# Three raw tiles and seven pairs of weight parts where one stream runs, and the next stage's first weights split on VectorE

## The chip, the cores and the metric

The kernel runs on one core of one Trainium2 chip. The metric is the device time of one execution in microseconds (us), the median of several runs. The matmul engine is TensorE (PE in the profile), the elementwise engines are VectorE (DVE), ScalarE (ACT) and GpSimd (POOL), and SyncE (SP) issues the loads of weights.

## The reference, cut to what matters

Two transformer blocks follow each other on `x` (512 tokens of 1024 features). Each has two layers, and each layer has two halves: token mixing, then a feed-forward. Every half has the same outline, and the change touches its joints:

```python
# first block, layer i (even: window and neighbourhood attention, odd: differential attention)
hx = hx + gx1 * yx                                    # yx = mixed @ w_out
hx = hx + gx2 * _mlp(_modulate(hx, norm2_g[i], sx2, cx2), mlp_w1[i], mlp_w2[i])
if with_ctx:                                          # layer 0 alone: a second stream, the context
    hc = hc + gc1 * yc
    hc = hc + gc2 * _mlp(_modulate(hc, norm2_g[i], sc2, cc2), mlp_w1[i], mlp_w2[i])
...
return _rms_norm(hx, final_g)                         # first block's end
# second block, layer l
h = _rmsnorm(x, norm1_w[l]) * (1.0 + sc1) + sh1
x = x + g1 * _token_mixers(h, w_in[l], ..., w_out[l])
h = _rmsnorm(x, norm2_w[l]) * (1.0 + sc2) + sh2
x = x + g2 * _conv_ffn(h, w_up[l], conv_f_w[l], w_down[l])
```

So a product (`@ w_out`, `@ w_down`, `@ mlp_w2`) ends in a residual add, the sum is normalised and modulated, and the next product (`@ mlp_w1`, `@ w_in`, `@ w_up`) starts from that. The norm needs all 1024 features of a token.

## The kernel before

Activations lie transposed: 8 chunks of 128 features by 512 tokens. A product in fp32 is made of three matmuls per chunk (`mm3`, L147 to L149): weights and activations are both split into a high part and a low part, and hi·hi, hi·lo and lo·hi are added in PSUM. A weight block of 1024 by 128 is loaded into a raw tile (`wraw`, 4 KB a partition), ScalarE writes its high part (`whi`, L129) and another engine subtracts for the low part (`wlo`, L130): VectorE, unless `weight()` is given another engine. A block is 24 matmuls of 512 columns. `whi` and `wlo` together are called a pair here. The pool of weights has a fixed number of raw tiles and of pairs; SP's load into a raw tile waits until the split that last used it is done, and a split waits until the matmuls that last used the pair are done.

`out_half` opens such a pool (`b.weights(env.wx, ...)`, L1489) while the last blocks of a layer's out-projection are still to be computed. The pool lasts through the feed-forward of that layer and the first blocks of the layer behind it. Loads of the modulation's weights (`w_ada`, used by VectorE at L181) take raw tiles of it too.

A joint of two stages is cut into two segments of 256 tokens, so that the norm of one can run beside products of the other:

- `down()` computes its last four blocks (three in the out-projection of the second block) segment by segment. Each output goes from PSUM into the residual `hx` (L154 on VectorE). After the four of segment 0, `norm` of segment 0 starts, while PE computes segment 1's four outputs.
- `norm`: squares on ScalarE (L213), added up on POOL (five) and VectorE (two, L218), a mean by matmul (`ms`, L224), a first root on ScalarE (`nr`, L232), a Newton step on VectorE (L233, L234, L235), then per chunk of features `nw` on VectorE (L242), the high part `axh` on ScalarE (L243) and the low part `axl` on VectorE (L244). At the end of the first block the final norm comes on top (L263 to L272, and a second Newton step).
- `first_chunks()` takes the first four blocks of the next product (called f0 to f3 below; g0, g1, ... are the blocks behind them), all four on segment 0 and then all four on segment 1, with `norm` of segment 1 between. The four are split with GpSimd as the engine.

There are five such joints with one stream: **A**, odd layer's out-projection to its MLP; **B**, that MLP to the first mixers (with the final norm); **C** and **E**, the mixers' out-projection to the conv FFN of layers 0 and 1; **D**, the first conv FFN to the second mixers. Which instruction stands where on an engine is decided by a scheduler when the program is built; each engine then runs its list in order.

Of the kernel before, what the change touches and what calls it, by code (L numbers as in the profile page):

```python
# [49 lines left out]
def segments(streams):  # L50
    return [(s, slice(i, i + SEG)) for s in reversed(streams) for i in range(0, s.n, SEG)]


class Build:
# [115 lines left out]
    def ada(self, w, bias, chunks, outs):  # L170

        nc = self.nc

        loaded = []

        def chunk(j):
            if loaded:
                raw, i = loaded.pop()
                for c, out in outs:
                    junk = self.tile(self.adap, [P, D], BF16, "adaj")  # L180
                    nc.vector.tensor_tensor_reduce(junk, raw, c, 1.0, self.vec(bias)[:, i:i + 1], ALU.mult, ALU.add,  # L181
                                                   out[:, i:i + 1])
            if j is not None:
                raw = self.wtile("wraw").rearrange("p a b -> p (a b)")
                nc.sync.dma_start(raw, self.io[w][j])
                loaded.append((raw, j))

        self.bg += [lambda j=j: chunk(j) for j in [*chunks, None]]
# [57 lines left out]
    def norm(self, pool, pp, s, sl, mod, outs, i, final=None):  # L246


        nc = self.nc
        scale, shift = mod  # L250
        h = s.h[:, :, sl]
        chunk = lambda k: h[:, k]
        acc = self.squares(pool, SEG, chunk, sq=f"sq{i}", pool_adds=5)
        if final is not None:
            acc2 = self.squares(pool, SEG, chunk, sq=f"sr{i}", pool_adds=5, scale=final)
        yield
        ms = self.mean(pp, acc, SEG)
        if final is not None:
            ms2 = self.mean(pp, acc2, SEG)
        r = self.newton(pool, ms, SEG)  # L260
        if final is not None:
            m = self.tile(pool, [P, SEG], F32, "nms")
            nc.vector.tensor_tensor(m, r, r, op=ALU.mult)  # L263
            nc.vector.tensor_tensor(m, m, ms2, op=ALU.mult)
            r2 = self.newton(pool, m, SEG)
            nc.vector.tensor_tensor(r2, r2, r, op=ALU.mult)
        for k in range(KC):
            hi, lo = outs[s.key][k]
            self.scaled(pool, h[:, k], r if final is None else r2, scale[:, k:k + 1], shift[:, k:k + 1], hi[:, sl], lo[:, sl])
        if final is not None:  # L270
            for k in range(KC):
                nc.vector.scalar_tensor_tensor(h[:, k], h[:, k], final[:, k:k + 1], r, op0=ALU.mult, op1=ALU.mult)  # L272
# [83 lines left out]
def first_chunks(b, pp, srcs, parts, streams, norm):  # L356


    ws = [b.weight(src, e=b.nc.gpsimd) for src, _ in srcs]
    ps = [{s.key: b.tile(pp, [P, T], F32, "dd") for s in streams if s.key in keys} for _, keys in srcs]  # L360
    for s, sl in segments(streams):
        for w, p in zip(ws, ps):
            if s.key in p:
                b.mm3(p[s.key][:, sl], w, parts[s.key], sl=sl)
            if norm:
                norm = norm()
    return [{k: v[:, :T if k == "x" else TC] for k, v in p.items()} for p in ps]


def down(b, pp, src, ops, streams, gates, kc=KC, ms=range(KC), after=None):  # L370


    ms = list(ms)
    full = ms[:-TAIL] if after else ms
    for m in full:
        w = b.weight(src(m), kc)
        for s in streams:
            ps = b.tile(pp, [P, T], F32, "dd")[:, :s.n]
            b.mm3(ps, w, ops[s.key], range(kc))
            b.add(s, m, slice(0, s.n), ps, gates[s.key])  # L380
    ws = [(m, b.weight(src(m), kc)) for m in ms[len(full):]]
    then = None
    for i, (s, sl) in enumerate(segments(streams) if ws else ()):
        for m, w in ws:
            ps = b.tile(pp, [P, T], F32, "dd")[:, :SEG]
            b.mm3(ps, w, ops[s.key], range(kc), sl)
            b.add(s, m, sl, ps, gates[s.key])
            if then:
                then = then()
        then = after(i, s, sl)  # L390
    return then
# [12 lines left out]
def mlp(b, pp, layer, a, norm, hset, streams, gates):  # L404

    nc, io = b.nc, b.io
    keys = [s.key for s in streams]
    up = lambda j: io[f"mlp_w1_{layer}"][j]
    first = first_chunks(b, pp, [(up(j), keys) for j in range(TAIL)], a, streams, norm)
    ctx = ExitStack()  # L410
    mt = b.pool(ctx, "mt", hset.side)
# [35 lines left out]
class EvenAttention:  # L447
# [6 lines left out]
    def load(self):  # L454

        b, ip = self.b, self.ip
        nc, io = b.nc, b.io
        b.rope_tables(b.cp)
        for n, w in (("maskA", 3 * P), ("maskB", 7 * P)):
            self.mask[n] = b.tile(ip, [P, w], F32R, n)  # L460
            for o in range(0, w, TA):
                m = slice(o, min(o + TA, w))
                raw = b.tile(ip, [P, TA], F32, "raw")[:, :m.stop - o]
                nc.sync.dma_start(raw, io[n][:, m])
                nc.scalar.copy(self.mask[n][:, m], raw)
        self.sink = b.tile(ip, [P, 8], F32, "sink")
        nc.sync.dma_start(self.sink, io["a_sink"].broadcast_to([P, 8]))
# [841 lines left out]
def conv_ffn(b, pp, l, a, norm, hset, streams, gates):  # L1309
    nc, io = b.nc, b.io  # L1310
    cw = b.vec(f"conv_f_w_{l}")
    up = lambda ch: io[f"w_up_{l}"][ch]
    chs = (0, NFF, 1, NFF + 1)
    first = dict(zip(chs, first_chunks(b, pp, [(up(ch), ["x"]) for ch in chs], a, streams, norm)))
    ctx = ExitStack()
    ft = b.pool(ctx, "ft", hset.side)
# [158 lines left out]
def out_half(b, env, w_out, ops, slots, streams, gates, mods, conds=(), order=range(KC), load=None, ada=None):  # L1475


    early = []
    for m, ps in enumerate(slots):
        w = b.weight(w_out[m])  # L1480
        for key, p in ps.items():
            b.mm3(p, w, ops[key], order)
    env.att.close()
    if load:
        load()
    streams = streams()
    env.new = b.open_set(env.other, [s.key for s in streams])
    env.wx, env.pdx = ExitStack(), ExitStack()
    b.weights(env.wx, b.nm("wd"), 4, 4, env.other)  # L1489
    for m, ps in enumerate(slots):  # L1490
        for s in streams:
            b.add(s, m, slice(0, s.n), ps[s.key], gates[s.key])
    env.ppx.close()
    env.pp = b.pool(env.pdx, "pd", space=PSUM)
    b.hold = 16
    env.wax.close()
    env.cond = None
    if conds:
        env.cond, c = b.open_cond(env.ins.side, conds)
        ada(*c)  # L1500
    rest = lambda after: down(b, env.pp, lambda m: w_out[m], ops, streams, gates, ms=range(len(slots), KC), after=after)
    return streams, *norms(b, env.pp, env.new, mods, streams, env.ins.side, rest)


def norms(b, pp, pset, mods, streams, side, rest, final=None):

    out = {}
    ctx = ExitStack()
    pool = b.pool(ctx, "nrm", side)
    b.bufs.update({"nr0": 2, "nt": 2})  # L1510

    def norm(i, s, sl):
        if not out:
            out.update(pset.all([s.key for s in streams]))
        steps = b.norm(pool, pp, s, sl, mods[s.key], out, i, final)
        next(steps)
        return lambda: next(steps, None)

    last = rest(norm)

    def complete():
        last()
        ctx.close()

    return out, complete


def next_layer(b, env, rest, mods, streams, srcs, final=None):

    a, norm = norms(b, env.pp, env.new, mods, streams, env.ins.side, rest, final)  # L1530
    first = first_chunks(b, env.pp, srcs, a, streams, norm)
    env.ins.close()
    env.wx.close()
    env.ins = env.new
    return a, first
# [26 lines left out]
def program(tc, io):  # L1562
    with ExitStack() as left:
# [10 lines left out]
        def ada(cx, cc):  # L1574
            b.ada("ada_w1", "ada_b1", range(16), [(cx, modx), (cc, modc)])
            b.ada("ada_w1", "ada_b1", range(16, 48), [(cx, modx)])

        streams, a, norm = out_half(b, env, io["even_w_out"], ops, slots, lambda: [b.c, b.x], g1, n2, ["c", "c_ctx"],
                                    load=lambda: b.open_h(left, io["xT"], io["ctxT"]), ada=ada)
        rest = mlp(b, env.pp, 0, a, norm, env.ins, streams, g2)  # L1580
# [8 lines left out]
        n2, g2 = b.modulation(modx, "norm2_g1", 1)  # L1589
        mod = b.tile(b.cp, [P, 48], F32, "mod2_0")  # L1590
        streams, a, norm = out_half(b, env, io["odd_w_out"], ops, slots, lambda: [b.x], {"x": gx1}, {"x": n2}, ["c_2"],
                                    ada=lambda c: b.ada("w_ada_0", "b_ada_0", range(48), [(c, mod)]))
        rest = mlp(b, env.pp, 1, a, norm, env.ins, streams, {"x": g2})
# [66 lines left out]
```

## Time and profile before

| what | value |
|---|---|
| median of 3 runs | 3237.75 us (3232.91 to 3242.6) |
| profiled execution: its own time, its span | 3238.63 us, 3236.6 us |
| busy share of the span: PE, DVE, ACT, POOL | 95%, 66%, 41%, 12% |
| mean granted TensorE clock | 0.983 of full speed |

Times inside the span are counted in us from its start. A busy share is an average over stages with different limits; the rows below are of single stretches. In a row of the timeline, `x3` means that three neighbouring instructions are put together, and a bracket gives the engine's idle time before it and what ended it. `out<-in` are the program's names.

### The profile page before, as it was taken

To read this page: it belongs to the slowest core of one execution; us is meant where nothing else is said; L and a number is where in the kernel's file an instruction comes from. 1 tells how busy PE (TensorE), PEld (TensorE's weight loads), DVE (VectorE), ACT (ScalarE), POOL (GpSimd) and SP (SyncE) were. 2 spreads that over 40 slices of the span, in tenths; PEclk is the share of its full clock that TensorE was granted. 3 is DMA by queue.
4 is the path that set the end of the run, shared out by engine and by line. 5 is a ranking of instruction groups with operands and counts; after the bars stand their busy time and mean duration, and the time that the engine had idled before them with its cause. 6 is when DMAs were issued, how large, how long until landed. Compare 5 with 4: busy or idle time off the path is not lost.

```text
span 3236.6 us, 46233 instructions
## 1 busy us (share of the span) xinstructions
PE 3059.5 (95%) x18168; PEld 2509.2 (78%) x18168; DVE 2131.1 (66%) x3745; ACT 1338.0 (41%) x2343; POOL 393.0 (12%) x434
## 2 busy tenths in 40 slices
PE   7999999999999999899998889899999899899998
PEld 5776888888888777788887666688888666688887
DVE  6656565544457667556657997586766897764545
ACT  4656431221335555432334444542334345543423
POOL 0000100000021111200003332200002422210000
PEclk9999999999999999899999999999999999999999
DMA  6322324434302222156641222246652222323332
GB/s 235 101 75 86 131 86 124 130 124 124 110 22 77 53 59 79 66 163 189 188 156 53 71 74 66 92 134 189 191 176 66 71 80 66 105 74 96 98 96 61
DMA packets 100330, 342.65 MB, mean 106 GB/s; under 512 B 12176, under 2 KB 15888, under 8 KB 97040
## 3 DMA queue, kind: packets, MB, share of 16 engines
q1 hardware_dynamic: 93840, 325.53, 31.7%
q0 software_dynamic: 5120, 11.01, 1.6%
q8 instruction: 143, 2.34, 0.3%
q10 hardware_dynamic: 1152, 3.15, 0.3%
q14 instruction: 75, 0.61, 0.1%
HBM read 326.54 MB, written 2.10 MB: 102 GB/s over the span
## 4 chain that ended last, share of the span: by engine, by line
PE 46%; DVE 15%; ACT 2%; DMA 2%; issue 2%; POOL 0%; DVEq 0%; POOLq 0%; ACTq 0%; SPq 0%
PE dd L148 11%; PE dd L147 11%; PE dd L149 11%; DVE qs L1155 3%; DVE rk L1167 2%; PE d L148 2%; PE d L147 2%; PE d L149 2%; DVE wlo L130 1%; DMA K<-K 1%; PE o L1098 1%; DVE AD L1186 1%; DVE nw L242 1%; DMA wraw<-in_w_ada 1%; PE o L1250 1%
## 5 line engine op out<-in xcount | busy, mean ns | idle before, releaser
L148 PE MATMUL dd<-axl,whi 128*128 128x512 f32 (+1 forms) x2728 | 979.4, 360 | 12.7 <-DVE axl L244 11.3
L147 PE MATMUL dd<-axh,whi 128*128 128x512 f32 (+1 forms) x2728 | 978.9, 360 | 12.6 <-ACT axh L243 12.3
L149 PE MATMUL dd<-axh,wlo 128*128 128x512 f32 (+1 forms) x2728 | 976.9, 359 | 0.0
L129 ACT CAST whi<-wraw 128x1024 fp32r<-128x1024 f32 (+1 forms) x388 | 402.8, 1042 | 1010.7 <-PE dd L148 747.5
L130 DVE TENSOR_TENSOR wlo<-wraw,whi 128x1024 fp32r<-128x1024 f32 (+1 forms) x361 | 444.2, 1234 | 335.8 <-ACT whi L129 326.3
L148 PEld LDWEIGHTS dd<-axl,whi 128*128 128x128 f32 x2728 | 520.2, 191 | 92.1 <-DVE axl L244 14.2
L147 PEld LDWEIGHTS dd<-axh,whi 128*128 128x128 f32 x2728 | 519.9, 191 | 90.5 <-ACT axh L243 14.6
L149 PEld LDWEIGHTS dd<-axh,wlo 128*128 128x128 f32 x2728 | 520.4, 191 | 76.5
L218 POOL TENSOR_TENSOR sq<-sq,sq 128x256 f32<-128x256 f32 x90 | 73.0, 819 | 1851.7 <-ACT sq L213 1788.2
L181 DVE CUSTOM_DVE_ANT_0 adaj<-wraw,cond,vecs 128x1024 bf16<-128x1024 f32 x160 | 205.3, 1283 | 136.5 <-DMA wraw<-in_ada_w 87.1
L147 PE MATMUL d<-axh,whi 128*128 128x512 f32 x664 | 275.3, 415 | 12.0 <-ACT axh L129 9.8
L148 PE MATMUL d<-axl,whi 128*128 128x512 f32 x664 | 273.1, 411 | 1.8 <-DVE axl L130 1.8
L149 PE MATMUL d<-axh,wlo 128*128 128x512 f32 x664 | 270.8, 408 | 1.1 <-DVE wlo L130 1.1
L1168 POOL TENSOR_TENSOR rf<-rf 64x256 f32<-64x256 f32 x192 | 160.4, 835 | 388.2 <-DVE rk L1167 357.1
L154 DVE SCALAR_TENSOR_TENSOR hx<-dd,mod,hx 128x512 f32<-128x512 f32 (+1 forms) x113 | 72.7, 645 | 164.8 <-PE dd L149 164.7
L147 PE MATMUL dd<-ach,whi 128*128 128x256 f32 x568 | 160.7, 283 | 0.0
L148 PE MATMUL dd<-acl,whi 128*128 128x256 f32 x568 | 160.6, 283 | 0.0
L149 PE MATMUL dd<-ach,wlo 128*128 128x256 f32 x568 | 160.5, 282 | 0.0
L147 PEld LDWEIGHTS d<-axh,whi 128*128 128x128 f32 x664 | 126.2, 190 | 41.0 <-ACT axh L129 11.4
L148 PEld LDWEIGHTS d<-axl,whi 128*128 128x128 f32 x664 | 126.3, 190 | 31.6 <-issue 4.9
L149 PEld LDWEIGHTS d<-axh,wlo 128*128 128x128 f32 x664 | 126.4, 190 | 27.5 <-DVE wlo L130 2.3
L328 PE MATMUL s<-K,Q 128*128 128x256 f32 (+1 forms) x336 | 116.4, 357 | 21.8 <-DMA K<-K 13.6
(364 smaller groups left out, 4691.2 us busy)
## 6 DMA issues: line engine op xcount, KB each, us to landing
wraw<-in_mlp_w SPq DMA_DIRECT2D x128, 512.0 KB, 3.5
wraw<-in_w_ada SPq DMA_DIRECT2D x96, 512.0 KB, 4.0
wraw<-in_w_up SPq DMA_DIRECT2D x88, 512.0 KB, 3.5
wraw<-in_w_in SPq DMA_DIRECT2D x56, 512.0 KB, 3.5
wraw<-in_ada_w SPq DMA_DIRECT2D x48, 512.0 KB, 3.6
adaw<-in_ada_wb SPq DMA_DIRECT2D x16, 1024.0 KB, 4.8
wraw<-in_w_down SPq DMA_DIRECT2D x32, 512.0 KB, 3.6
wraw<-in_odd_w_in SPq DMA_DIRECT2D x24, 512.0 KB, 3.6
```

Of the source, the lines that this page charges most:

```text
L129: self.nc.scalar.copy(hi, src)
L130: (e or self.nc.vector).tensor_tensor(lo, src, f32(hi), op=ALU.subtract)
L147: mm(ps, hi[:, k], xh[:, sl], start=first, stop=False)
L148: mm(ps, hi[:, k], xl[:, sl], start=False, stop=False)
L149: mm(ps, lo[:, k], xh[:, sl], start=False, stop=last)
L154: self.nc.vector.scalar_tensor_tensor(h, ps, gate[:, m:m + 1], h, op0=ALU.mult, op1=ALU.add)
L181: nc.vector.tensor_tensor_reduce(junk, raw, c, 1.0, self.vec(bias)[:, i:i + 1], ALU.mult, ALU.add, out[:, i:i + 1])
L218: e.tensor_tensor(acc, acc, s2, op=ALU.add)
L328: mm(ps, q[:, slot, toks], k1[:, keys], start=True, stop=False)
L1155: nc.vector.tensor_tensor(halves(qs[r], m)[1 - d], halves(Q[h][r], m)[1 - d], halves(F[h][r], m)[1 - d], op=ALU.mult)
L1167: nc.vector.tensor_tensor(k[d], k[d], whole[1 - d], op=ALU.mult)
L1168: nc.gpsimd.tensor_tensor(f[1 - d], f[1 - d], whole[d], op=ALU.mult)
```

## The change

A pool that `out_half` opens with one stream has 3 raw tiles and 7 pairs, where it had 4 and 4 (17 tiles in place of 12); with two streams it keeps 4 and 4. With one stream `first_chunks` leaves the engine of the low parts at its default, VectorE.

```diff
@@ def first_chunks(b, pp, srcs, parts, streams, norm):
-    ws = [b.weight(src, e=b.nc.gpsimd) for src, _ in srcs]
+    ws = [b.weight(src, e=None if len(streams) == 1 else b.nc.gpsimd) for src, _ in srcs]
@@ def out_half(b, env, w_out, ops, slots, streams, gates, mods, conds=(), order=range(KC), load=None, ada=None):
-    b.weights(env.wx, b.nm("wd"), 4, 4, env.other)
+    b.weights(env.wx, b.nm("wd"), *((3, 7) if len(streams) == 1 else (4, 4)), env.other)
```

GpSimd's list has 20 instructions fewer (323 to 303 rows) and VectorE's 20 more (3492 to 3512). This is VectorE's list at joint A; `wlo_13043`, `13049`, `13055` and `13061` are the low parts of f0 to f3, `wlo_13339`, `13378` and `13417` those of g0 to g2, and L154 is the residual add of the out-projection:

```order
+L154 SCALAR_TENSOR_TENSOR hx_3937<-s_12555,modx_932_3767,hx_3937 128x512 x2
 L130 TENSOR_TENSOR wlo_12727<-wraw_12724,whi_12726 128x1024
-L154 SCALAR_TENSOR_TENSOR hx_3937<-s_12555,modx_932_3767,hx_3937 128x512 x2
+L130 TENSOR_TENSOR wlo_13043<-wraw_13040,whi_13042 128x1024
+L130 TENSOR_TENSOR wlo_13049<-wraw_13046,whi_13048 128x1024
 L154 SCALAR_TENSOR_TENSOR hx_3937<-s_12556,modx_932_3767,hx_3937 128x512
+L130 TENSOR_TENSOR wlo_13055<-wraw_13052,whi_13054 128x1024
```

f0 to f2 are now split ahead of the joint. A little further down the same list, where segment 0's Newton step stands:

```order
 L154 SCALAR_TENSOR_TENSOR hx_3937<-dd_12873,modx_932_3767,hx_3937 128x256
+L130 TENSOR_TENSOR wlo_13061<-wraw_13058,whi_13060 128x1024
 L233 TENSOR_TENSOR nt_12902<-nr_2590_12901 128x256
 L234 SCALAR_TENSOR_TENSOR nt_12902<-ms_12899,eps_62,nt_12902 128x256
 L154 SCALAR_TENSOR_TENSOR hx_3937<-dd_12939,modx_932_3767,hx_3937 128x256
 L235 SCALAR_TENSOR_TENSOR nr_2590_12901<-nt_12902,nr_2590_12901 128x256
+L130 TENSOR_TENSOR wlo_13339<-wraw_13336,whi_13338 128x1024
 L242 SCALAR_TENSOR_TENSOR nw_12907<-hx_3937,msc_2526_12557,nr_2590_12901 128x256
```

f3 stands ahead of the Newton step and g0 between it and the first `nw`; g1 and g2 stand around the second addition of squares of segment 1 (L218), ahead of that segment's L233. At C and E, where the out-projection's tail has three blocks, f0 to f3 are all split ahead of the joint, and g0, g1 and g2 stand ahead of L233, between L235 and L242, and between the two additions. At B and D only f3 stands inside the joint, ahead of L233 (D: ahead of an L154 and L233), and no g does.

GpSimd's list at joint A keeps the additions of squares alone (`sq_2580` is segment 0's sum, `sq_2603` segment 1's):

```order
 L218 TENSOR_TENSOR sq_2580_12850<-sq_2580_12850,sq_2585_12864 128x256
-L130 TENSOR_TENSOR wlo_13043<-wraw_13040,whi_13042 128x1024
 L218 TENSOR_TENSOR sq_2603_13017<-sq_2603_13017,sq_2607_13028 128x256
-L130 TENSOR_TENSOR wlo_13049<-wraw_13046,whi_13048 128x1024
 L218 TENSOR_TENSOR sq_2603_13017<-sq_2603_13017,sq_2608_13031 128x256
-L130 TENSOR_TENSOR wlo_13055<-wraw_13052,whi_13054 128x1024
-L130 TENSOR_TENSOR wlo_13061<-wraw_13058,whi_13060 128x1024
```

The four splits have left it, and the additions stand closer together.

## Rows read from the trace of the kernel before

Columns of rows 1 to 3: the stretch and its length, the busy time (and instructions) of PE, PE's weight loads, DVE, ACT and POOL, then the granted clock, the DMA engines' share and GB/s.

**Rows 1.** Stretches: a steady stage, then joints A, B, C, D, E.

```profile
1386.30:1697.40 311.10, 309.70 (x1347) 252.45 (x1346) 187.79 (x245) 96.17 (x127) 6.94 (x8) 1.00 0.58 178
...
1330.30:1386.30 56.00, 51.61 (x390) 49.98 (x389) 33.80 (x59) 26.67 (x48) 19.88 (x14) 0.91 0.17 57
1697.40:1760.00 62.60, 53.49 (x393) 51.57 (x391) 48.73 (x97) 25.64 (x51) 25.38 (x29) 0.89 0.05 18
2088.50:2134.50 46.00, 43.55 (x342) 42.63 (x341) 31.66 (x58) 24.28 (x43) 15.10 (x10) 0.96 0.21 70
2459.20:2507.90 48.70, 43.49 (x341) 42.33 (x339) 33.12 (x65) 21.97 (x40) 14.90 (x10) 0.96 0.13 47
2836.00:2881.90 45.90, 43.41 (x342) 42.49 (x341) 31.67 (x58) 23.39 (x42) 15.03 (x10) 0.96 0.19 58
```

**Rows 2.** Stretches at half clock: A, B, B, C, D, E.

```profile
1358.31:1368.55 10.24, 7.01 (x29) 6.23 (x29) 7.58 (x11) 1.75 (x6) 4.24 (x2) 0.50 0.31 102
1723.54:1733.78 10.24, 6.46 (x25) 5.58 (x25) 10.24 (x15) 5.45 (x10) 6.12 (x5) 0.50 0.00 0
1747.43:1750.84 3.41, 3.41 (x18) 3.41 (x18) 3.41 (x10) 1.40 (x4) 0.00 (x0) 0.50 0.00 0
2109.24:2112.66 3.42, 3.42 (x18) 3.42 (x18) 3.42 (x10) 2.22 (x6) 2.87 (x1) 0.50 0.09 34
2481.30:2484.71 3.41, 3.03 (x14) 3.03 (x15) 3.41 (x6) 1.42 (x3) 1.91 (x1) 0.50 0.40 154
2856.76:2860.17 3.41, 3.41 (x19) 3.41 (x18) 3.41 (x9) 2.22 (x6) 3.05 (x1) 0.50 0.02 8
```

**Rows 3.** A stretch of 256-column matmuls without a gap.

```profile
2459.50:2471.02 11.52, 11.52 (x98) 11.47 (x97) 4.65 (x9) 4.02 (x9) 3.12 (x5) 1.00 0.16 49
```

**Rows 4.** Timeline of DVE at A: start, duration, line; segment 0, then 1.

```profile
1349.37 2.46 DVE L235 SCALAR_TENSOR_TENSOR nr<-nt,nr 128x256 f32<-128x256 f32 x1
...
1358.56 4.27 DVE L244 SCALAR_TENSOR_TENSOR axl<-nw,modx,axh 128x256 fp32r<-128x256 f32 x2
...
1367.13 0.43 DVE L235 SCALAR_TENSOR_TENSOR nr<-nt,nr 128x256 f32<-128x256 f32 x1
...
1373.41 0.89 DVE L244 SCALAR_TENSOR_TENSOR axl<-nw,modx,axh 128x256 fp32r<-128x256 f32 x2 [0.18 <-ACT axh L243]
```

**Rows 5.** Timeline of POOL at A.

```profile
1349.16 2.38 POOL L130 TENSOR_TENSOR wlo<-wraw,whi 128x1024 fp32r<-128x1024 f32 x1
1351.51 0.92 POOL L218 TENSOR_TENSOR sq<-sq,sq 128x256 f32<-128x256 f32 x1
1355.07 7.49 POOL L130 TENSOR_TENSOR wlo<-wraw,whi 128x1024 fp32r<-128x1024 f32 x2 [2.65 <-DVE nw L242]
```

**Rows 6.** Timeline of DVE at D, segment 0.

```profile
2474.59 6.64 DVE L242 SCALAR_TENSOR_TENSOR nw<-hx,msc,nr 128x256 f32<-128x256 f32 x5
```

**Rows 7.** Timeline of DVE at C, segment 0.

```profile
2104.48 2.43 DVE L235 SCALAR_TENSOR_TENSOR nr<-nt,nr 128x256 f32<-128x256 f32 x1
...
2112.90 2.62 DVE L244 SCALAR_TENSOR_TENSOR axl<-nw,mod,axh 128x256 fp32r<-128x256 f32 x2
```

**Rows 8.** Timeline of DVE at B, segment 0: the first and last of six.

```profile
1713.05 2.36 DVE L233 TENSOR_TENSOR nt<-nr 128x256 f32<-128x256 f32 x1 [0.85 <-ACT nr L232]
...
1730.99 2.59 DVE L272 SCALAR_TENSOR_TENSOR hx<-hx,gs,nr 128x256 f32<-128x256 f32 x1
```

**Rows 9.** Timeline of PE at D and B: two of the longest waits.

```profile
2481.68 0.58 PE L148 MATMUL dd<-axl,whi 128*128 128x256 f32 x1 [3.60 <-DVE axl L244]
...
1746.56 0.50 PE L147 MATMUL dd<-axh,whi 128*128 128x256 f32 x2 [2.72 <-ACT axh L243]
```

**Rows 10.** Groups by line and form: splits on VectorE and casts on ScalarE.

```profile
L130 DVE TENSOR_TENSOR wlo<-wraw,whi 128x1024 fp32r<-128x1024 f32 x345 | 429.0, 1246 | 320.9 <-ACT whi L129 311.4
L129 ACT CAST whi<-wraw 128x1024 fp32r<-128x1024 f32 x372 | 389.4, 1051 | 989.0 <-PE dd L148 728.3 <-PE d L148 237.0 <-PE s L148 8.9
```

**Rows 11.** The page, loads: KB each, median us from issue to landing.

```profile
wraw<-in_w_ada SPq DMA_DIRECT2D x96, 512.0 KB, 4.0
```

## Prediction

> **What bounds the kernel now.** I read the page first: PE is busy 95% of the span, so what can be gained lies where PE waits or runs at a lower clock. Next I read stretches [rows 1]. In the steady stage PE is busy 309.70 of 311.10 us at a granted clock of 1.00, and a matmul of 512 columns starts every 311.10 / 1347 = 0.231 us, so nothing that shortens another engine's work there shortens the kernel. The five joints are different: 56.0, 62.6, 46.0, 48.7 and 45.9 us, with a clock of 0.89 to 0.96. PE's idle time in them is length less busy time: A 4.4, B 9.1, C 2.45, D 5.2, E 2.5 us, together 23.7. The clock takes the rest. There are six stretches at 0.50, the lower of the two levels [rows 2]; half of the work done there was lost: 7.01/2 = 3.5 in A, (6.46 + 3.41)/2 = 4.9 in B, 1.7, 1.5 and 1.7 in C, D and E, together 13.4. So the joints hold 37.0 us that are not PE's own work (A 7.9, B 14.0, C 4.2, D 6.7, E 4.2). As a check, a matmul of 256 columns at full clock takes 11.52/98 = 0.12 us [rows 3], so the joints' 1808 [rows 1] would need 213 to 217 us, and they took 259: the 37.0 and some 5 to 9 us more in which matmuls start a little late without an idle engine, of which I count none.
>
> Then I asked what PE waits for there. It is the norm's products: the longest waits end with `axl` or `axh` [rows 9]. The timeline of VectorE says why these are late. At A the Newton step L235 took 2.46 us in segment 0 and 0.43 in segment 1; two L244 took 4.27 and then 0.89 [rows 4]. On GpSimd a split of f0 to f3 runs from 1349.16 to 1351.54, and two from 1355.07 for 7.49 us [rows 5]: the slow VectorE operations end within 0.3 us of those splits. The same at D, where five L242 took 6.64 us (five at 0.43 are 2.15) [rows 6], at C [rows 7], and at B, where six rows of ten operations from L233 to L272 took 13.9 us for 4.3 [rows 8].
>
> A rule of the Trainium skill names this ("SBUF — State Buffer", Who interferes with whom): a VectorE instruction with two inputs in SBUF and a GpSimd instruction that reads SBUF exclude each other, and whichever has the shared port first blocks the other fully. The trace agrees: 2.46 against 0.43 us. The rule also speaks against a part of this change: 20 more VectorE splits, each with two SBUF inputs, now meet GpSimd's additions of squares; taken alone it would give back up to one addition per meeting.
>
> **The change part by part.** *GpSimd's 20 splits go.* What they delayed on VectorE falls away. *VectorE's 20 splits come.* One is 1.25 us [rows 10]. Those ahead of the joints (f0 to f2 in A, B, D; f0 to f3 in C, E) lie beside a PE that runs from full pairs; VectorE is busy 188 of 311 us in such a stage [rows 1]. They cost nothing while that cover lasts; without it, 17 times 1.25 = 21 us at most. f3 stands where VectorE waited for `nr` anyway. That leaves g0, g1 and g2 inside the chain in A, C and E. *3 raw tiles in place of 4.* A raw tile's turn is load, cast and split: 4.0 + 1.05 + 1.25 = 6.3 us [rows 10, 11]. While a modulation weight holds one tile, the other two alternate, so each may take two blocks' matmul time, 2 × 24 × 0.231 = 11.1 us. Nothing waits: 0. *7 pairs in place of 4* let the next blocks be split ahead; PE in the steady stage has no idle time to give back: 0.
>
> By joint:
>
> - **A.** L235 is 2.0 us faster and the two L244 3.4, while g0 adds 1.25 ahead of the first `nw`. Idle 4.4 and half clock 3.5 go; I leave about 1.0 for g0 and for g1, g2 ahead of segment 1. Saves 6.9.
> - **B.** The ten operations shrink by 13.9 − 4.3 = 9.6 us. That ends the waits of segment 0, but segment 1's norm starts behind L272 and the last L154 on VectorE, so the end of the joint moves only with VectorE's chain. The first matmul of segment 1 stood at 1746.56 [rows 9]; it moves 9.6 earlier less 1.4 for f3 and for meetings with GpSimd's additions (four there, 0.92 each [rows 5], of which I charge about half, with f3 mostly hidden). A gap ahead of segment 1 and a half-clock stretch behind it stay. Saves 8.2.
> - **C and E.** L235 gives 2.0 and g0 takes 1.25; the wait of about 2 us shrinks below the shortest behind which these joints show a drop of the clock, which gives 1.7. Two L244 are 1.7 faster, but g1 and g2 put 2.5 ahead of segment 1's Newton step, while PE gets there 2.4 earlier: I charge 0.45. Saves 0.75 + 1.7 − 0.45 = 2.0 each.
> - **D.** Five L242 take 2.15 and not 6.64, and no g stands in the chain. The 3.60 us wait [rows 9] and the 1.5 of half clock go, about 0.5 stays. Saves 6.2.
>
> The sum is 6.9 + 8.2 + 2.0 + 6.2 + 2.0 = 25.3. From the profiled execution's own 3238.63 us that gives 3213.3. The median of the runs is 0.9 lower, which is inside their spread, so I say **3213**.
>
> Two prices are not in the trace. How much VectorE's splits lose to GpSimd's additions: between nothing and 0.92 each, for some 20 additions that fall in the joints, 0 to 18 us, if every one fell in the chain; nearer the low end, since VectorE's slack ahead of the joints takes most, and the sum charges 1 to 3. And how short a gap still lowers the clock: between none of these gaps and all of them, 0 to 8.4 us (A 3.5, C 1.7, D 1.5, E 1.7).
>
> **The rivals.**
>
> - *The clock still falls.* Shorter gaps remain in A, C, D, E, and each is followed by half clock as before. For it: C and E fell with no more than 2.5 us of idle time in the whole joint. Against it: the sum leaves some 1 us of idle time in each of these joints, under half of that. The saving is 25.3 − 8.4 = 17: 3222.
> - *VectorE becomes the bound of the joints.* g0, g1, g2 in A, C and E are 9 × 1.25 = 11.2 us, of which the sum charges about 4.5; and meetings with additions take another 4. The saving is 25.3 − 6.7 − 4 = 14.6: 3224. VectorE is busy 33 to 34 of 46 to 56 us in A, C, D, E [rows 1], which leaves room overall, though not in the chain.
> - *The change doesn't do what it says.* The VectorE operations were slow for another reason, the additions of squares among them, and stay slow. Only the chance of smaller gaps remains: 3232 to 3239. Against it: at A the slow operations end at 1351.8 and 1362.8, GpSimd's splits at 1351.5 and 1362.6 [rows 4, 5], and nothing else that ends there is in sight.
> - *Slower: three raw tiles starve the split.* If a tile's turn, 6.3 us by the rows, exceeds 11.1 us because SP's loads queue behind one that waits for its tile, PE waits for every block while modulation weights are loaded. At a turn of 12.1, that is 0.5 us a block for 96 blocks, the number of those loads: 48 less the 25 saved, 3261. It decides from a turn of about 11.6 (96 × 0.25 = 24). The margin of 4.8 us speaks against it.
> - *More than forecast:* all 37.0 us go: 3202.
>
> **How the numbers follow.** Forecast (3207 to 3218) 0.50; clock falls 0.17; VectorE bound 0.14; no effect 0.11; starved 0.05; all gone 0.03. A measurement of this kernel can tell about 0.3%, 10 us, from no change. Faster takes the forecast, the first rival, nearly all of the second and the last: 0.83. Same: 0.12. Slower: 0.05. The range leaves out the ends of the no-effect and starved cases, and holds the first two rivals with some of their spread: 3202 to 3229.
>
> **What would show it.** Right: at all five joints no VectorE operation of segment 0 over 1.5 times that of segment 1, GpSimd's busy time there down to a few us, the clock 1.00 in A, C, D, E, and 0.50 only at B behind a gap of 4 to 5 us ahead of segment 1. The joints' lengths should be about 49, 54.5, 44, 42.5 and 44 us, the steady stages unchanged. Wrong: waits of PE for `whi` or `wlo` in the steady stages; `axl` still late though GpSimd is idle; or additions that grow to the length of a split, with VectorE's operations still waiting for them.

## The result and the profile after

The changed kernel takes 3204.28 us (median of 4 runs, 3202.15 to 3205.91) against 3238.21 us of the kernel before beside it: a ratio of 0.990 with an interval of 0.9886 to 0.9914. The forecast was 3213, range 3202 to 3229. The profiled execution took 3202.81 us, its span is 3201.0 us, the mean clock 0.990.

These are the stretches of the changed kernel that answer to [rows 1] and [rows 2]: joints A to E, the steady MLP, and the only half-clock stretch that the joints still have. The stretches begin and end at the matmuls with the same number as in the kernel before; cut so, the joints of before are 56.1, 63.2, 46.1, 49.3 and 45.9 us long.

```profile
1327.24:1375.37 48.13, 47.79 (x391) 47.11 (x390) 34.21 (x65) 27.51 (x50) 9.03 (x10) 1.00 0.35 113
1684.75:1740.51 55.76, 50.55 (x392) 48.95 (x390) 40.81 (x98) 23.28 (x50) 15.30 (x25) 0.97 0.08 29
2068.06:2110.45 42.39, 41.86 (x343) 41.16 (x342) 29.72 (x59) 23.45 (x42) 5.13 (x7) 1.00 0.19 63
2434.60:2477.18 42.58, 41.53 (x340) 40.80 (x338) 27.90 (x66) 19.73 (x39) 6.34 (x10) 1.00 0.10 34
2804.19:2846.44 42.25, 41.65 (x342) 40.98 (x341) 29.71 (x59) 22.52 (x41) 5.09 (x7) 1.00 0.17 52
1375.37:1684.75 309.38, 309.19 (x1346) 252.41 (x1345) 187.99 (x245) 96.34 (x128) 6.88 (x8) 1.00 0.58 177
1726.98:1730.39 3.41, 3.41 (x16) 3.08 (x15) 3.41 (x10) 1.51 (x4) 0.00 (x0) 0.50 0.00 0
```

PE's idle time in A, C, D and E is now 0.3, 0.5, 1.05 and 0.6 us, at a clock of 1.00 throughout. The joints became 7.9, 7.4, 3.7, 6.75 and 3.7 us shorter, 29.5 together. B alone keeps a gap and a half-clock stretch. This is VectorE's timeline at A, segment 0 and the start of segment 1, the answer to [rows 4]:

```profile
1345.72 0.42 DVE L235 SCALAR_TENSOR_TENSOR nr<-nt,nr 128x256 f32<-128x256 f32 x1
1346.05 1.22 DVE L130 TENSOR_TENSOR wlo<-wraw,whi 128x1024 fp32r<-128x1024 f32 x1
1347.19 1.76 DVE L242 SCALAR_TENSOR_TENSOR nw<-hx,msc,nr 128x256 f32<-128x256 f32 x3
...
1353.62 0.87 DVE L244 SCALAR_TENSOR_TENSOR axl<-nw,modx,axh 128x256 fp32r<-128x256 f32 x2
...
1358.08 0.43 DVE L233 TENSOR_TENSOR nt<-nr 128x256 f32<-128x256 f32 x1 [0.26 <-ACT nr L232]
```

L235 fell from 2.46 to 0.42 us and two L244 from 4.27 to 0.87, as in segment 1 of before. g0's split (1.22) stands in the chain, and three L242 take 1.76 where segment 1 has 1.28: 0.5 us, while an addition of squares runs on GpSimd. L233, L234 and L235 aren't slowed. GpSimd's list from 1338 to 1372 us is now this, against [rows 5]; its second addition took 1.47 us, twice the first, beside g0's split and the first L242:

```profile
1344.82 0.73 POOL L218 TENSOR_TENSOR sq<-sq,sq 128x256 f32<-128x256 f32 x1 [9.16 <-ACT sq L213]
1346.40 1.47 POOL L218 TENSOR_TENSOR sq<-sq,sq 128x256 f32<-128x256 f32 x1 [0.85 <-ACT sq L213]
```

PE's longest wait in the joints, at B ahead of segment 1, answers to the row of B in [rows 9]:

```profile
1726.00 0.38 PE L147 MATMUL dd<-axh,whi 128*128 128x256 f32 x1 [3.91 <-ACT axh L243]
```

The profiled executions differ by 35.8 us. The joints explain 29.5. The steady MLP behind A adds 1.7, of which one wait of 0.95 us for a low part of the activations was in the kernel before. The rest, some 4.6, lies mostly ahead of joint A (3.1) or in the mixers, in code that the change leaves alone. A second profiled execution of the changed kernel took 3206.76 us with the same joints within 0.25 us, and 2.6 us more in the first mixers, where TensorE ran 10.24 us at a clock of 0.50 (2029.70 to 2039.94) and in the first profile 3.41 (2030.77 to 2034.18). So a remainder of that size is what two executions differ by.

### The profile page after: what moved, and what is told of

Same layout as the page of the kernel before. It is cut to its first block, busy times and chain, and to the rows that moved or that the text cites. A ratio compares the mean times of both kernels' runs of the same rounds, so it can differ in the third digit from the quotient of the medians.

```text
span 3201.0 us, 46331 instructions
## 1 busy us (share of the span) xinstructions
PE 3044.2 (95%) x18168; PEld 2495.8 (78%) x18168; DVE 2120.4 (66%) x3765; ACT 1337.8 (42%) x2343; POOL 336.9 (11%) x414
## 5 line engine op out<-in xcount | busy, mean ns | idle before, releaser
L148 PE MATMUL dd<-axl,whi 128*128 128x512 f32 (+1 forms) x2728 | 973.4, 358 | 0.5 <-DVE axl L244 0.3
L149 PE MATMUL dd<-axh,wlo 128*128 128x512 f32 (+1 forms) x2728 | 970.9, 357 | 0.0
L130 DVE TENSOR_TENSOR wlo<-wraw,whi 128x1024 fp32r<-128x1024 f32 (+1 forms) x381 | 464.1, 1222 | 345.6 <-ACT whi L129 332.6
L148 PEld LDWEIGHTS dd<-axl,whi 128*128 128x128 f32 x2728 | 515.7, 189 | 77.5 <-DVE axl L130 1.0
L149 PEld LDWEIGHTS dd<-axh,wlo 128*128 128x128 f32 x2728 | 515.4, 189 | 76.6
L218 POOL TENSOR_TENSOR sq<-sq,sq 128x256 f32<-128x256 f32 x90 | 75.5, 849 | 1987.0 <-ACT sq L213 1922.1
L148 PE MATMUL d<-axl,whi 128*128 128x512 f32 x664 | 272.8, 411 | 1.8 <-DVE axl L130 1.8
L149 PE MATMUL d<-axh,wlo 128*128 128x512 f32 x664 | 270.7, 408 | 1.1 <-DVE wlo L130 1.1
L154 DVE SCALAR_TENSOR_TENSOR hx<-dd,mod,hx 128x512 f32<-128x512 f32 (+1 forms) x113 | 72.8, 646 | 165.7 <-PE dd L149 165.7
L148 PE MATMUL dd<-acl,whi 128*128 128x256 f32 x568 | 160.5, 283 | 0.0
L149 PE MATMUL dd<-ach,wlo 128*128 128x256 f32 x568 | 160.4, 282 | 0.0
L148 PEld LDWEIGHTS d<-axl,whi 128*128 128x128 f32 x664 | 126.2, 190 | 31.8 <-issue 4.9
L149 PEld LDWEIGHTS d<-axh,wlo 128*128 128x128 f32 x664 | 126.3, 190 | 27.4 <-DVE wlo L130 2.3
```

The source lines that it names most:

```text
L130: (e or self.nc.vector).tensor_tensor(lo, src, f32(hi), op=ALU.subtract)
L148: mm(ps, hi[:, k], xl[:, sl], start=False, stop=False)
L149: mm(ps, lo[:, k], xh[:, sl], start=False, stop=last)
L154: self.nc.vector.scalar_tensor_tensor(h, ps, gate[:, m:m + 1], h, op0=ALU.mult, op1=ALU.add)
L218: e.tensor_tensor(acc, acc, s2, op=ALU.add)
```

## The experiments

Two theories stood against each other. **Theory 1:** VectorE's norm operations wait while a GpSimd split runs, and the change keeps splits out of their way. **Theory 2:** seven pairs let the next stage's weights be split earlier, and that is the gain, whatever engine does it. Later runs ask what the raw tiles and the pairs are worth, and what holds B.

Length of the joints in us, cut as above, each in one profiled execution, and medians of runs:

| kernel | A | B | C | D | E | median us |
|---|---|---|---|---|---|---|
| before | 56.1 | 63.2 | 46.1 | 49.3 | 45.9 | 3236.6 to 3238.7 |
| changed | 48.1 | 55.8 | 42.4 | 42.6 | 42.3 | 3204.28 |
| dve_splits_4_4 | 48.2 | 59.4 | 42.6 | 43.9 | 42.4 | 3209.76 |
| pool_splits_3_7 | 48.6 | 57.5 | 42.4 | 42.9 | 42.2 | 3209.85 |
| pool_reads_late | 54.7 | 61.7 | 48.7 | 49.3 | 48.7 | 3237.03 |
| pool_writes_late | 48.9 | 56.5 | 43.1 | 43.3 | 43.0 | 3208.38 |
| pairs_5 | 48.1 | 58.4 | 42.4 | 43.1 | 42.3 | 3217.11 |
| raw4_pairs6 | 48.1 | 56.1 | 42.4 | 43.1 | 42.3 | 3207.66 |
| late_final | 48.1 | 53.2 | 42.4 | 42.6 | 42.3 | 3198.37 |
| late_final_tied | 48.1 | 50.7 | 42.4 | 42.6 | 42.2 | 3199.17 |

**One half of the change: the engine alone (dve_splits_4_4).**

```diff
-    b.weights(env.wx, b.nm("wd"), *((3, 7) if len(streams) == 1 else (4, 4)), env.other)
+    b.weights(env.wx, b.nm("wd"), 4, 4, env.other)
```

> Only the engine of the first four splits is changed (VectorE); the pool keeps 4 raw tiles and 4 pairs. Theory 1 (VectorE's norm operations wait for GpSimd's splits): VectorE is free of them as in the changed kernel, and its list has splits at the same places inside joints A, C and E; at B and D two or three splits more stand in the chain, 1.25 us each, so 3204 + 3 + 3 = 3210 us (3206 to 3216). Theory 2 (the gain comes from weights that are split earlier, which takes the 7 pairs): the four splits stay inside the joints, so little is gained, 3230 to 3239. A sum of two halves would be near 3221.

3209.76 us, a ratio to before of 0.9916 (0.9901 to 0.9931). That is theory 1's number; that it fits to the microsecond is luck, since the parts were 3 and 3 for B and D, and B loses 3.7 us and D 1.3. A, C and E are as in the changed kernel. Theory 2 falls as an explanation of the whole: the splits here are as late as before (the first two inside A start 15.4 and 18.8 us after its beginning, before 15.5 and 18.8).

**The other half: the pool alone (pool_splits_3_7).**

```diff
-    ws = [b.weight(src, e=None if len(streams) == 1 else b.nc.gpsimd) for src, _ in srcs]
+    ws = [b.weight(src, e=b.nc.gpsimd) for src, _ in srcs]
```

> Only the pool is changed (3 raw tiles, 7 pairs); GpSimd keeps the first four splits. Theory 1 (VectorE's norm operations wait for GpSimd's splits): at C and E all four splits now lie ahead of the joint, so these gain what the changed kernel gained, 3.7 us each; at A, B and D the last one or two splits still meet the norm, so about half of the 22 us there: 3238 - 7 - 11 = 3220 us (3212 to 3228), and slow VectorE operations end with those splits. Theory 2 (earlier weights, whatever the engine): 3204 to 3208, as the changed kernel.

3209.85 us, 0.9915 (0.9901 to 0.993): 5.6 us from the changed kernel, outside both ranges, since I took more splits to meet the norm than do. GpSimd's timeline at A shows it:

```profile
1326.42 4.77 POOL L130 TENSOR_TENSOR wlo<-wraw,whi 128x1024 fp32r<-128x1024 f32 x2 [54.34 <-ACT whi L129]
...
1334.99 2.40 POOL L130 TENSOR_TENSOR wlo<-wraw,whi 128x1024 fp32r<-128x1024 f32 x1
...
1344.09 2.39 POOL L130 TENSOR_TENSOR wlo<-wraw,whi 128x1024 fp32r<-128x1024 f32 x1 [4.47 <-ACT whi L129]
```

Only the fourth is near the norm, and meets its first operation alone, which takes 0.93 us in place of 0.43:

```profile
1345.83 0.93 DVE L233 TENSOR_TENSOR nt<-nr 128x256 f32<-128x256 f32 x1 [2.26 <-ACT nr L232]
```

So the pool alone also takes the splits out of the norm's way, by time and not by engine. Either half gives five sixths of the gain, and the two don't add up. This run by itself fits both theories; what separates them is the run above and the next ones.

**GpSimd's reads put back, in the wrong place (pool_reads_added).** `self.one` says that one stream runs, `self.padd` is GpSimd's last addition of squares, and `behind` puts an instruction behind another one on its engine's list.

```diff
...
+        if self.one and i == 0:
+            d = self.tile(pool, [P, 512], F32, "dum")
+            last = nc.gpsimd.memset(d, 0.0)
+            self.behind(last, self.padd)
+            for _ in range(6):
+                ins = nc.gpsimd.tensor_tensor(d, d, d, op=ALU.subtract)
+                self.behind(ins, last)
+                last = ins
```

> The changed kernel, and in each of the five joints, behind GpSimd's last addition of squares of segment 0, six GpSimd subtractions of 128x512 on a tile of their own that nobody reads (some 7 us). No VectorE instruction, weight or pair is moved. Theory 1: VectorE's operations with two inputs in SBUF wait again, by up to the length of a subtraction each, and half or more of the gain goes: 3218 to 3236 us. Theory 2: nothing changes, 3202 to 3207.

3205.36 us, no change, against theory 1's number. GpSimd's timeline at A says why it tells nothing:

```profile
1338.62 6.76 POOL L264 TENSOR_TENSOR dum<-dum 128x512 f32<-128x512 f32 x6
```

The six end at 1345.4, and VectorE's first norm operation there starts at 1346.9. A twin with fourteen memsets in the same place:

> As the run with the added subtractions, but fourteen GpSimd memsets of 128x512 in their place (some 7 us too), which read nothing. Theory 1 in its form with reads: VectorE doesn't wait, 3202 to 3210 us. If any GpSimd work beside the norm is what hurts (its additions of squares of segment 1 come later behind it, or any access counts), it comes out like the subtractions, 3218 to 3236.

3203.9 us, for the same reason no evidence.

**GpSimd's reads beside the norm (pool_reads_late).**

```diff
...
         r = self.newton(pool, ms, SEG)
+        if self.one and i == 0:
+            d = self.tile(pool, [P, 512], F32, "dum")
+            nc.gpsimd.tensor_tensor(d[:, :SEG], r, r, op=ALU.mult)
+            nc.gpsimd.tensor_tensor(d[:, SEG:], r, r, op=ALU.mult)
+            for _ in range(6):
+                nc.gpsimd.tensor_tensor(d, d, d, op=ALU.subtract)
```

> The changed kernel with six GpSimd subtractions of 128x512 on an own tile again, but tied to the result of segment 0's Newton step (two GpSimd products of it come first), so that they run beside the operations L242 and L244, about 8 us a joint. In the run with the subtractions further ahead they fell into a time in which VectorE waited anyway (until 1345.4, VectorE's L233 there at 1346.9), so it told nothing of the norm. Theory 1 (GpSimd's reads hold VectorE's two-input operations): those operations of segment 0 take 1.5 to 3 times as long, the gaps of PE and the half clock come back in most joints, 3218 to 3236 us. Theory 2 (the gain comes from early split weights): 3202 to 3208.

3237.03 us, a ratio to before of 1.0001 (0.9992 to 1.0011): the whole gain is gone, though the splits ahead of the subtractions are made as early and by the same engine as in the changed kernel. That the loss is as large as the gain is chance: the subtractions aren't the splits of before, and C and E come out 2.6 and 2.7 us longer than before, A and B 1.4 and 1.5 shorter. VectorE at A:

```profile
1347.77 2.47 DVE L243 SCALAR_TENSOR_TENSOR nw<-hx,msc,nr 128x256 f32<-128x256 f32 x3
1350.17 3.62 DVE L245 SCALAR_TENSOR_TENSOR axl<-nw,modx,axh 128x256 fp32r<-128x256 f32 x3
1353.71 3.61 DVE L243 SCALAR_TENSOR_TENSOR nw<-hx,msc,nr 128x256 f32<-128x256 f32 x3
1357.25 1.26 DVE L245 SCALAR_TENSOR_TENSOR axl<-nw,modx,axh 128x256 fp32r<-128x256 f32 x3
```

and GpSimd:

```profile
1349.93 7.12 POOL L267 TENSOR_TENSOR dum<-dum 128x512 f32<-128x512 f32 x6
```

(The added lines move L242 and L244 to L243 and L245.) While the six subtractions run, from 1349.93 to 1357.05, three VectorE operations take 3.6 us: one each 1.2, the length of one subtraction (7.12/6 = 1.19). Behind them three take 1.26 again.

**GpSimd's writes in the same place (pool_writes_late).**

```diff
-            for _ in range(6):
-                nc.gpsimd.tensor_tensor(d, d, d, op=ALU.subtract)
+            for _ in range(14):
+                nc.gpsimd.memset(d, 0.0)
```

> As the run before, with fourteen memsets of 128x512 in place of the six subtractions, behind the same two products. Theory 1 in its form with reads: only the two products of 128x256 meet VectorE (under 1 us a joint), 3203 to 3211 us. If any GpSimd work there hurts, 3218 to 3236.

3208.38 us, 0.9915 (0.99 to 0.993). GpSimd's memsets and, from VectorE's timeline, the operations beside them:

```profile
1349.18 8.12 POOL L267 MEMSET dum<- 128x512 f32 x14
```

```profile
1349.45 1.26 DVE L245 SCALAR_TENSOR_TENSOR axl<-nw,modx,axh 128x256 fp32r<-128x256 f32 x3
1350.64 1.27 DVE L243 SCALAR_TENSOR_TENSOR nw<-hx,msc,nr 128x256 f32<-128x256 f32 x3
```

As much GpSimd time, and VectorE isn't held at all. The 0.7 us a joint by which this run is behind is the price of the two products that come first: the first three L243 take 2.47 us at A in both runs, and 1.76 in the changed kernel. So it is GpSimd's reads, not its being busy.

**Two raw tiles (two_raw_7).**

```diff
-*((3, 7) if len(streams) == 1 else (4, 4))
+*((2, 7) if len(streams) == 1 else (4, 4))
```

> The changed kernel with 2 raw tiles in place of 3. The rival of starved splits, taken to its point: while a modulation weight holds one tile, one tile is left, whose turn of 4.0 + 1.05 + 1.25 = 6.3 us is longer than a block's 5.5 us of matmuls. If the reckoning of turns is right, PE waits about 0.8 us at each of some 90 blocks, +70 us, 3260 to 3300; with waits of the engines in the turn still more. If raw tiles don't matter even then, 3204.

3225.17 us, 21 above the changed kernel, where 56 to 96 were expected. All joints stay as in the changed kernel; the steady MLP grows from 309.4 to 322.5 us and the first conv FFN's from 324.15 to 330.7. The chain of waits of ScalarE in the steady MLP, of the changed kernel and then of this one (total us, times, longest):

```profile
ACT whi L129 <- PE dd L148: 167.9, 55, 4.6
...
ACT whi L129 <- DMA wraw<-in_mlp_w: 1.5, 1, 1.5
```

```profile
ACT whi L129 <- DMA wraw<-in_mlp_w: 154.2, 48, 5.7
...
ACT whi L129 <- PE dd L148: 9.3, 4, 3.8
```

With three raw tiles the casts wait for a pair, that is, they run as far ahead as pairs allow; with two they wait for the load. Yet PE isn't short of weights at each block: it has five waits in these two stages, 12.7 us together, for the activations' cast that stands behind such a weight cast on ScalarE's list, and 13.7 us at half clock. The longest on PE's timeline:

```profile
1678.94 0.80 PE L147 MATMUL dd<-axh,whi 128*128 128x512 f32 x1 [4.52 <-ACT axh L129]
```

**Five pairs (pairs_5)** and **four raw tiles with six pairs (raw4_pairs6).**

```diff
-*((3, 7) if len(streams) == 1 else (4, 4))
+*((3, 5) if len(streams) == 1 else (4, 4))   # pairs_5
+*((4, 6) if len(streams) == 1 else (4, 4))   # raw4_pairs6
```

> The changed kernel with 3 raw tiles and 5 pairs in place of 7: f0 alone is split ahead of joints A, B and D, f0 and f1 ahead of C and E; the splits at the places inside the joints are as many as before, of other blocks. Theory 1: A, C and E unchanged, B and D lose part of the 3.7 and 1.3 us by which the changed kernel is ahead of the one with 4 pairs: 3206 to 3208 us. Theory 2: nearly all of the pairs' gain goes, 3209 or more.

3217.11 us, 0.9943 (0.9928 to 0.9958): worse than four pairs with four raw tiles, which neither theory had. B loses 2.7 us, D 0.5, as theory 1 has it; but the first mixers behind B take 336.7 us, and 327.6 in the changed kernel. At their start PE waits for the mixers' first weight, and SP had issued its load late. PE and SP of this run, and SP of the changed kernel:

```profile
1749.57 0.80 PE L147 MATMUL d<-axh,whi 128*128 128x512 f32 x1 [3.41 <-ACT whi L129]
```

```profile
1744.74 0.80 SPq L135 DMA_DIRECT2D wraw<-in_w_in  x2
```

```profile
1734.23 0.80 SPq L135 DMA_DIRECT2D wraw<-in_w_in  x2
```

The load waits for the last low-part matmul of a block of the old pool (the releaser of its wait is PE L149), and is issued 0.8 us ahead of the end of joint B (1745.5); in the changed kernel it is 6.3 us ahead (1740.51). I take it from this wait that the mixers' raw tiles lie on memory of the old pool, and that the pool's size decides which tile lies there; no view shows the addresses. The wait of 3.41 us and the half clock that began in it (1748.50 to 1755.30, with PE busy 5.70, so 2.9 lost) are 6.3 of those 9.1 us. The rest isn't shown to come from the pairs: further down the mixers have 10.24 us at half clock (2042.04 to 2052.28) where the changed kernel has 3.41 in its first profile, and 10.24 in its second.

> 4 raw tiles and 6 pairs in place of 3 and 7, the splits on VectorE. If the third raw tile is enough (ScalarE's casts in the steady MLP wait for pairs, not for loads: 1.5 us in one wait for a load), the fourth brings nothing, and one pair fewer costs a part of B: 3204 to 3207. If three tiles already cost something in the steady stages, 4 are faster there: 3198 to 3202. If what 5 pairs lost (8.9 us behind B, where the mixers' first load waits until the memory that it takes is free) comes with any other layout, 3210 to 3216.

3207.66 us (3202.63 to 3209.32), 0.9909 (0.9892 to 0.9925), against 3205.39 (3200.7 to 3206.76) of the changed kernel beside it:

> The changed kernel once more, beside the next two: 3204 us (3201 to 3207) by every theory.

The runs overlap. B and D lose 0.4 and 0.5 us, the steady MLP is 309.2 against 309.4 us, the first conv FFN 324.2 in both. So a fourth raw tile buys nothing there, and doing with three costs nothing. Behind B the first mixers take 329.8 us against 327.6 in the changed kernel's first profile, with the same time at half clock. PE waits there for VectorE, whose first operation of the mixers had waited 4.67 us for a matmul of joint B (PE L148):

```profile
1741.43 0.47 PE L147 MATMUL d<-axh,whi 128*128 128x512 f32 x1 [1.87 <-DVE raw L1135]
```

So with this size too something at the start of the mixers comes late, though not a load.

**The rest of B (late_final, late_final_tied).** Segment 0's final scaling L272 (L273 in these runs) is written behind segment 1's norm; in the second run it is also tied there. At B both also have four buffers `nr0` in place of two.

```diff
         if final is not None:
+            yield True
             for k in range(KC):
-                nc.vector.scalar_tensor_tensor(h[:, k], h[:, k], final[:, k:k + 1], r, op0=ALU.mult, op1=ALU.mult)
+                ins = nc.vector.scalar_tensor_tensor(h[:, k], h[:, k], final[:, k:k + 1], r, op0=ALU.mult, op1=ALU.mult)
+                self.behind(ins, self.low)          # with `ins`: late_final_tied alone; self.low: the last L244
...
     def complete():
         last()
+        for steps in late:
+            next(steps, None)
         ctx.close()
```

> The changed kernel, and at joint B the eight L272 of segment 0 (the final norm's scaling of the residual, 3.3 us) are written behind segment 1's norm and not ahead of it. In the changed kernel PE still waits 3.91 us there for segment 1's first product, behind L272 and the last L154 on VectorE, and runs at half clock for 3.4 us. If that chain is what holds B: the gap falls to about 1 us and the half clock goes, 2.9 + 1.7 = 4.6 us less, 3199 to 3200. If ScalarE, GpSimd's additions or the mean hold segment 1's norm: 3203 to 3205.

3198.37 us (3196.13 to 3206.09). B is 53.2 us, 2.5 shorter, where 4.6 was expected: the gap shrank to 1.82 us, not to 1, and the half clock stayed (1723.31 to 1726.72).

```profile
1721.75 0.38 PE L147 MATMUL dd<-axh,whi 128*128 128x256 f32 x1 [1.82 <-ACT axh L243]
```

> As the run with the late final norm, but segment 0's eight L272 are tied behind segment 1's last L244 on VectorE's list. Written late alone, they were hoisted between segment 1's Newton steps, three of them (1.27 us) ahead of the first L233, and PE's gap was 1.82 us, with half clock behind it. Without them on that chain the first product of segment 1 should come 1.2 to 1.8 us earlier: a gap of 0 to 0.6 us, and no half clock, which is 1.7 us more; joint B 53.2 - 3 = 50 us, about 3196. If ScalarE's root and the mean are the rest of the chain, the gap stays above 1.3 us and half clock with it: 3198 to 3199. The eight L272 then stand ahead of the mixers' first VectorE operations (3 us); if these are needed at once, what B gains is lost there.

3199.17 us (3197.21 to 3201.42), where about 3196 was expected. B is 50.7 us, as expected, with a gap of 0.69 us and a clock of 1.00; but up to 3.7 us (a wait of 1.98 and half of 3.41) are lost at once behind it, the loss that the expectation named last. PE's timeline:

```profile
1721.21 0.38 PE L147 MATMUL dd<-axh,whi 128*128 128x256 f32 x1 [0.69 <-ACT axh L243]
...
1736.52 0.47 PE L147 MATMUL d<-axh,whi 128*128 128x512 f32 x1 [1.98 <-DVE raw L1137]
```

VectorE's sixteen scalings, eight of each segment, now run in one piece ahead of the mixers' first operations:

```profile
1726.74 6.42 DVE L273 SCALAR_TENSOR_TENSOR hx<-hx,gs,nr 128x256 f32<-128x256 f32 x16
...
1735.69 0.68 DVE L1137 TENSOR_TENSOR raw<-raw,dd 128x512 f32<-128x512 f32 x1
```

PE waits 1.98 us for L1137, and half clock follows (1738.28 to 1741.69). Both versions are ahead of the changed kernel by 5 to 7 us in their medians; of that only 2.5 us of the first are shown in the joint, and its slowest run, 3206.09, is within the changed kernel's. The second's 5.1 us at B are mostly given back in the first mixers (331.7 us for 327.6), so where it is faster isn't shown.

## Why the prediction was right, point by point

- *The number.* 3204.28 lies in the range, but below the 3207 to 3218 of the forecast itself, which had half the chance, and 2 us above the rival "more than forecast". The joints beat the sum by 4.2 us; another 4.4 lie outside the joints, where the sum had nothing.
- *What bounds the kernel.* Right. PE's waits and half clock in the joints were 37.0 us; 29.5 us of joint came back, and the steady stages kept their lengths within 2 us.
- *What PE waits for.* Right, and shown both ways: with splits moved by engine or by time the slow operations go, and with GpSimd reads put back beside the norm they return, with 32.8 us of loss. The rule of the Trainium skill ("SBUF — State Buffer", Who interferes with whom) that VectorE's two-input operations contend with GpSimd instructions that read SBUF, and not with those that only write it, agrees with the trace: 3.6 us for three operations beside subtractions, 1.26 beside memsets.
- *A, 6.9 forecast, 7.9 measured; D, 6.2 and 6.75.* Right. A's reserve of 1.0 for g0 to g2 wasn't needed: its gap is 0.32 us.
- *C and E, 2.0 forecast each, 3.7 measured.* The term that was mis-sized, 3.4 of the 4.2 us by which the joints beat the sum. The half clock's 1.7 came as forecast. Of PE's idle time I let 0.75 − 0.45 = 0.3 us go; at C it fell from 2.45 to 0.5. The first L242 starts 1.5 us sooner, not 0.75, because L233 was slow as well (0.94 us, now 0.42), which the sum left out; the split between L235 and L242 is g1 there, not g0, and costs its 1.2. With segment 1 there is no wait, so the 0.45 wasn't needed. L233 and PE's wait at C, before and after:

```profile
2102.71 0.94 DVE L233 TENSOR_TENSOR nt<-nr 128x256 f32<-128x256 f32 x1 [2.26 <-ACT nr L232]
...
2108.03 0.38 PE L147 MATMUL dd<-axh,whi 128*128 128x256 f32 x1 [2.00 <-ACT axh L243]
```

```profile
2082.25 0.42 DVE L233 TENSOR_TENSOR nt<-nr 128x256 f32<-128x256 f32 x1 [0.56 <-ACT nr L232]
...
2086.04 0.73 PE L147 MATMUL dd<-axh,whi 128*128 128x256 f32 x4 [0.47 <-ACT axh L243]
```

- *B, 8.2 forecast, 7.4 measured.* Right in kind: the gap ahead of segment 1 (3.91 us; 4 to 5 forecast) and the half clock of 3.41 us stay, and taking L272 off that chain shortens the gap to 1.82, and to 0.69 when it is kept off it. The first matmul of segment 1 comes 7.8 us sooner. The 1.4 that I took off for f3 and the additions is less than the half of four additions that I named (1.8); they cost VectorE 0.9 there, as below.
- *What would show it.* Most came: the clock, the lengths within 1.7 us, the steady stages, GpSimd's busy time (5 to 9 us, at B 15.3). But four VectorE operations of segment 0 are still over 1.5 times those of segment 1, each beside an addition of squares: the first L242 at A (0.97 us for 0.48) and at D (0.84), the first L233 at B (0.97 for 0.43) and an L234 there (0.84 for 0.48).
- *VectorE against GpSimd's additions, 1 to 3 us charged.* Right: these four operations lose 1.8 us together, 0.9 of it at B.
- *3 raw tiles for 4: nothing.* Right: a fourth bought nothing in the steady stages. The reckoning of a tile's turn gave the right side, but not the size when it was pushed to two tiles: 21 us and not 56 to 96. PE waits five times and not at each block, and for ScalarE's order; that blocks split ahead in pairs cover the rest is my reading, which no run shows.
- *7 pairs: nothing.* Wrong in the small: with VectorE's splits, seven pairs in place of four are worth 5.5 us between medians, 3.7 of it at B and 1.3 at D, where with four pairs f0 to f2 are split inside the joint too.
- *The rivals.* TensorE's clock fell in no joint but B. VectorE didn't become the bound of A, C, D or E; its busy time there was 31.7 to 33.8 us before, where that rival says 33 to 34. Splits didn't starve at three tiles: in the steady MLP ScalarE waited once for a load, 1.5 us.

The medians differ by 33.9 us, the joints by 29.5. Some 1 to 2 us lie in the steady MLP; for the last 2 to 3 us no place in the changed code is shown, and they are within what runs of one kernel differ by.

## What to carry to other kernels

An elementwise operation that takes 2 to 6 times its own length in one place and not in its twin is a sign to look at what another engine does at its end. GpSimd was cheap here only where VectorE had no two-input work on the path: splitting the weights there ahead of the joint, or on VectorE, each gave most of the gain alone. When a pool is resized, look at the next pool's first load too: two pairs fewer made that load 5.5 us later against the end of the joint. And before a difference of a few microseconds is put down to a change, look where it lies: here the half clock outside the joints differs that much between two executions of one kernel.

## What the runs showed of the hardware

- GpSimd memsets of 128x512 beside VectorE's two-input operations cost these nothing (1.26 us for three), GpSimd subtractions of the same shape made three take 3.6 us.
- Half clock behind a gap isn't a fixed price. In the one profile of each, a gap of 1.82 us (B in late_final) was followed by 3.41 us at 0.50, one of 0.69 us (late_final_tied) by none. The same matmul in the second mixers waits 2.93 or 2.94 us in all fourteen profiles, and five of them show half clock in it or within 2 us behind it, nine don't. The changed kernel itself is in both groups. These are the 5.43 us from the end of that wait on: the kernel before, the changed kernel, and the changed kernel's second profile (after_again), at 0.69, 1.00 and 0.50:

```profile
2582.57:2588.00 5.43, 5.43 (x18) 3.49 (x20) 4.86 (x10) 2.07 (x4) 1.12 (x1) 0.69 0.17 35
```

```profile
2551.13:2556.56 5.43, 5.30 (x24) 2.84 (x26) 4.86 (x10) 3.06 (x5) 1.12 (x1) 1.00 0.18 42
```

```profile
2552.96:2558.39 5.43, 5.43 (x14) 3.86 (x14) 4.86 (x10) 1.07 (x2) 1.12 (x1) 0.50 0.19 33
```
